# Token shift by ScalarE into PSUM, squares of the input norms in PSUM, the projection's low parts read back from DRAM, and a new order

## The chip, the cores and the metric

The kernel runs on one core of a Trainium2 chip. Five engines run their own instruction streams: TensorE (PE, with PEld for its weight loads), VectorE (DVE), ScalarE (ACT), GpSimd (POOL) and SyncE (SP), which issues the transfers of this kernel; sixteen DMA engines carry them out. The metric is the device time of one launch in microseconds (us). Three runs of the kernel before gave 2299.95, 2302.5 and 2308.67 us; their median is 2302.5 us.

## The reference

One layer of a hybrid decoder, for 1024 prompt tokens and 8 decode tokens that share the weights. D_MODEL is 1024, D_FF 2816, all in fp32. Cut to the parts in question:

```python
h = x + 0.5 * rmsnorm(swiglu(rmsnorm(x, n_ffn1_pre), ffn1_gate, ffn1_up, ffn1_down), n_ffn1_post)
u = rmsnorm(h, n_mix_pre)
proj = u @ w_in                       # 26 column tiles of 128
...                                   # group A: differential attention
shifted = concatenate([prev, pb[:, :-1]])
xs = pb + (shifted - pb) * mu_shift   # token shift of group B
...                                   # group B: RWKV-7 delta rule, 8 heads of 64
h = h + rmsnorm(concatenate([ya, yb]) @ w_out, n_mix_post)
h = h + 0.5 * rmsnorm(swiglu(rmsnorm(h, n_ffn2_pre), ffn2_gate, ffn2_up, ffn2_down), n_ffn2_post)
```

## The kernel before, in words

Activations stand transposed, features on partitions and tokens on the free axis. The tokens are worked in two halves of about 512. There are four FFN phases, called trunk0 to trunk3: trunk0 and trunk1 are the first FFN of halves 0 and 1, trunk2 and trunk3 the second FFN of halves 0 and 1. Between them lie, for each half, the input projection `proj` (w_in, 26 column tiles), the mixing work (`job`, `lora`, `attn`, `prep`, `fin`), the output projection (`out` for half 0, `outb` for half 1), and norms: a phase's `tail` is the norm and residual after it, `outn` the one after the output projection, `stats` and `pre` the one ahead of an FFN. `dec` and `decb` are the decode tokens' attention and state update; `decb` reads its state and operands as 64x512 pieces from DRAM (`decb_dreg<-Dd`).

Each fp32 product is three matmuls (`mm3`, L675): high weight by high input, high weight by low input, low weight by high input. `split` (L599) makes the two parts of a weight tile: ACT casts the high part, and DVE or POOL subtracts it from the raw tile for the low part. With `kept` the low part is written to DRAM in half 0 and read from there in half 1, in place of the subtraction (`aside`, L615). Before, this is done for parts of the FFN weights and for w_out (`Lo`), named in `LOWS` (L99). The projection's tiles use buffers w0 and w1 in half 0, and w2 and w3, taken in turn, in half 1; a tile's buffer is given to the tile after the next when its last matmul is done. In half 1 a tile is 24 matmuls of 512 columns; of each three, the third needs the low part.

`stats` (L794) sums the squares of eight feature tiles: ACT squares into a buffer `sqs` (one buffer), DVE or POOL adds it to an accumulator, a matmul with ones sums over the partitions, ACT takes the root and DVE the reciprocal (`rstd`). The token shift (in `s_mix`'s streams) is a POOL subtraction of a 128x512 tile and a DVE multiply-add.

The order is not the program's. Generators ("streams") put instructions; `Kern.run` (L475) lists them for each engine by earliest start, ties by a late time, and every engine then runs its list in that order. The late times come from dry passes (`latest`, L564): each pass runs the list, works back from its end, and gives the next pass its late times; `PASSES` is how many. `BIAS` moves the late times of a stream by a number of microseconds. Since all engine work is issued through one helper, every row of the profile has its line, L317 (L320 after); streams are told apart by the tiles' names. PSUM banks: trunk uses m0 and m1, projections m2 and m3, norms a small bank "dec" or "aux".

## Time and profile before

The profiled execution took 2294.3 us, its span 2292.3; that is 8.2 us (0.36%) under the median of the three runs.

| engine | busy, us | share of the span |
|---|---|---|
| PE | 2228.0 | 97% |
| PEld | 1985.3 | 87% |
| DVE | 1556.5 | 68% |
| ACT | 1078.0 | 47% |
| POOL | 1021.6 | 45% |

The rows of the trace give an engine's instructions in order of time with, in brackets, the idle time ahead of one and what ended it. PEclk is the granted TensorE clock as a share of the full one. The DMA share is the mean busy share of the sixteen DMA engines. Idle time of an engine other than PE costs nothing by itself.

### The profile page before, as it was taken

What the parts mean: (1) busy time and instruction counts of PE and PEld (TensorE: products, weight loads), DVE (VectorE), ACT (ScalarE), POOL (GpSimd) and SP (SyncE); (2) the same over time, 40 slices, a digit from 0 to 9 for tenths busy, and PEclk for the clock granted to TensorE, in tenths of its full rate; (3) what the DMA queues carried; (4) which work ended last, traced back from release to release, by engine and by line L of the source; (5) the groups of instructions that cost most, each with busy time, mean ns of one, the idle gap of its engine ahead of it and who ended that gap; (6) DMA issues with size and microseconds to landing.
All of it is one profiled execution on the core that took longest, in us unless ns stands there. A gap on an engine that the chain in (4) does not pass through costs nothing. (4 is left out here: it accounts for less than half of the span.)

```text
span 2292.3 us, 42829 instructions
## 1 busy us (share of the span) xinstructions
PE 2228.0 (97%) x15857; PEld 1985.3 (87%) x15857; DVE 1556.5 (68%) x3545; ACT 1078.0 (47%) x2231; POOL 1021.6 (45%) x846
## 2 busy tenths in 40 slices
PE   8999999999999999999899999999999999999998
PEld 7999999799887778988787867777788888999998
DVE  5477988756766687477866367665667356777776
ACT  5433443634354365434552145443665556544444
POOL 3344565534343566356543124333443254544443
PEclk9999999999999999999899999999999999999999
DMA  6423334344334576655679643324745847544543
GB/s 205 132 86 100 102 93 130 104 146 140 109 113 108 170 228 204 218 151 151 194 200 225 169 138 114 111 75 121 205 122 168 273 145 249 148 114 130 148 138 111
DMA packets 476295, 343.15 MB, mean 150 GB/s; under 512 B 82457, under 2 KB 424061, under 8 KB 476088
## 3 DMA queue, kind: packets, MB, share of 16 engines
q1 hardware_dynamic: 475480, 338.82, 50.8%
q8 instruction: 125, 2.05, 0.4%
q0 software_dynamic: 320, 1.08, 0.1%
q14 instruction: 82, 0.67, 0.1%
q10 hardware_dynamic: 288, 0.52, 0.1%
HBM read 278.98 MB, written 61.38 MB: 148 GB/s over the span
## 5 line engine op out<-in xcount | busy, mean ns | idle before, releaser
L317 PE MATMUL trunk_m<-trunk_xl,wts_w 128*128 128x256 f32 (+2 forms) x2700 | 459.4, 321 | 6.9 <-DVE trunk_xl L317 6.2
L317 POOL TENSOR_TENSOR wts_w<-wts_raw,wts_w 128x1024 fp32r<-128x1024 f32 (+2 forms) x162 | 314.4, 1948 | 318.1 <-ACT wts_w L317 279.4
L317 PE MATMUL trunk_m<-pre_X,wts_w 128*128 128x512 f32 (+3 forms) x2400 | 439.9, 335 | 5.7 <-POOL wts_w L317 2.8
L317 PEld LDWEIGHTS trunk_m<-trunk_xl,wts_w 128*128 128x128 f32 x2700 | 382.3, 189 | 42.3 <-DVE trunk_xl L317 7.9
L317 PEld LDWEIGHTS trunk_m<-pre_X,wts_w 128*128 128x128 f32 x2400 | 352.6, 190 | 48.2 <-issue 6.8
L317 PE MATMUL trunk_m<-pre_T,wts_w 128*128 128x512 f32 (+3 forms) x1848 | 362.8, 347 | 5.2 <-DVE trunk_xl L317 2.4
L317 ACT CAST wts_w<-wts_raw 128x1024 fp32r<-128x1024 f32 (+2 forms) x293 | 244.2, 848 | 237.9 <-PE trunk_m L317 162.1
L317 PEld LDWEIGHTS trunk_m<-pre_T,wts_w 128*128 128x128 f32 x1848 | 286.9, 190 | 43.7 <-issue 3.8
L317 DVE TENSOR_TENSOR trunk_xl<-trunk_xl,trunk_m 128x256 f32<-128x256 f32 (+2 forms) x351 | 165.8, 489 | 77.3 <-PE trunk_m L317 76.1
L317 PE MATMUL proj_m<-tail_xl,lin_w 128*128 128x256 f32 (+1 forms) x1248 | 168.5, 290 | 2.3 <-POOL lin_w L317 1.9
L317 PEld LDWEIGHTS proj_m<-tail_xl,lin_w 128*128 128x128 f32 x1248 | 155.6, 190 | 11.3 <-issue 7.0
L317 POOL TENSOR_TENSOR trunk_xl<-trunk_t,trunk_xl 128x512 fp32r<-128x512 f32 (+3 forms) x86 | 94.5, 1100 | 149.9 <-ACT trunk_xl L317 149.7
L317 PE MATMUL proj_m<-tail_T,lin_w 128*128 128x512 f32 (+1 forms) x672 | 153.1, 386 | 4.9 <-ACT tail_T L317 3.8
L317 PEld LDWEIGHTS proj_m<-tail_T,lin_w 128*128 128x128 f32 x672 | 122.6, 192 | 33.2 <-ACT tail_T L317 4.2
L317 DVE TENSOR_TENSOR wts_w<-wts_raw,wts_w 128x1024 fp32r<-128x1024 f32 (+2 forms) x101 | 108.1, 1071 | 35.1 <-ACT wts_w L317 34.4
L317 POOL TENSOR_TENSOR wts_w<-wts_lraw,wts_w 128x512 fp32r<-128x512 f32 x44 | 66.4, 1512 | 53.5 <-ACT wts_w L317 46.9
L317 ACT CAST wts_w<-wts_lraw 128x512 fp32r<-128x512 f32 x94 | 55.9, 617 | 64.7 <-DMA wts_lraw<-in_ffn_down_dram 33.4
L317 POOL TENSOR_TENSOR lin_w<-lin_raw,lin_w 128x1024 fp32r<-128x1024 f32 x19 | 45.9, 2417 | 79.4 <-ACT lin_w L317 69.7
L317 DVE TENSOR_TENSOR trunk_t<-trunk_g,trunk_m 128x512 f32<-128x512 f32 (+2 forms) x75 | 42.1, 562 | 53.4 <-PE trunk_m L317 50.7
L317 POOL TENSOR_TENSOR mix_T<-mix_T 128x512 f32<-128x512 f32 x32 | 38.6, 1207 | 79.2 <-DMA mix_T<-PT 54.6
L317 PE MATMUL trunk_aux<-trunk_xl,wts_w 128*128 128x256 f32 (+1 forms) x516 | 71.5, 283 | 0.0
L317 PE MATMUL trunk_m<-comb_T,wts_w 128*128 128x260 f32 x540 | 69.8, 283 | 0.0
(645 smaller groups left out, 4273.9 us busy)
## 6 DMA issues: line engine op xcount, KB each, us to landing
wts_raw<-in_ffn_gate_dram SPq DMA_DIRECT2D x88, 512.0 KB
wts_raw<-in_ffn_up_dram SPq DMA_DIRECT2D x58, 512.0 KB
wts_raw<-in_ffn_down_dram SPq DMA_DIRECT2D x56, 384.0 KB
wts_raw<-in_ffn_down_dram SPq DMA_DIRECT2D x29, 512.0 KB
lin_raw<-in_w_in_dram SPq DMA_DIRECT2D x26, 512.0 KB
wts_w<-Ld SPq DMA_DIRECT2D x22, 512.0 KB
mix_T<-PT SPq DMA_DIRECT2D x37, 256.0 KB
Ld<-wts_w SPq DMA_DIRECT2D x24, 384.0 KB
```

Of the source, the lines that this page charges most:

```text
L317: o = Op(eng, lambda: fn(*a, **k), st)
```

## The change

Six things change. (1) `PASSES` goes from 2 to 4, and the `BIAS` table loses ten entries and gets two; so every engine's order may change. (2) `MIX`: the token shift's first half is an ACT instruction that writes (1 - mu) times the tile into PSUM, and DVE adds mu times the shifted tile to it; POOL's subtraction is gone. A small tile `rest_mu` is computed once. (3) `SQP`: `stats` writes its squares into a PSUM tile and adds all of them on DVE. (4) `LOWS` has "in": the projection's 26 low parts (512 KB each) are written to DRAM in half 0 (`Li<-lin_w`) and read in half 1 (`lin_w<-Li`), in place of 26 subtractions. (5) The stream `lora` is given the PSUM bank "dec". (6) `SWAP` is 0, so its branches do nothing.

```diff
-PASSES = 2
-BIAS = {"trunk2": 310, "outn3": -60, "outb0": 30, "pre2": -3, "outn0": -30, "rows0": -30, "job00": -10, "job03": 10, "stats0": 10, "dec0": 10, "wts3": 3, "pre3": -30, "mix1": -60, "lora1": 3, "attn11": 3, "tail2": 3}
+PASSES = 4
+BIAS = {"trunk2": 300, "outn3": -60, "outb0": 30, "pre2": -3, "pre1": -60, "rope0": 10}
 SHIFT = {}
+SWAP = 0
+MIX = 1
+SQP = 1
...
-LOWS = (1, "out")
+LOWS = (1, "in", "out")
...
+        self.rest_mu = self.T(self.const, [P, NB], "rmu")
+        nc.vector.tensor_scalar(self.rest_mu, self.vecs("mu_shift"), -1.0, 1.0, ALU.mult, ALU.add)
...
         for k in range(KT):
-            self.square_sum(rb, src[k], k, self.tmp(*tmp, rb.shape[-1]), **kw)
+            if SQP:
+                self.square_sum(rb, src[k], k, self.ps2()[:, :rb.shape[-1]], engines=("vector",))
+            else:
+                self.square_sum(rb, src[k], k, self.tmp(*tmp, rb.shape[-1]), **kw)
         self.rstd(rb)
...
-        self.spawn(self.s_lora(pool, half), "lora", 0)
+        self.spawn(self.s_lora(pool, half), "lora", 0, "dec")
...
+        if MIX:
+            part = self.ps2()
+            nc.scalar.activation(part, E[:, 1:], AF.Copy, scale=self.rest_mu[:, m:m + 1])
+            nc.vector.scalar_tensor_tensor(out, E[:, 0:HS], self.vec("mu_shift", m), part, ALU.mult, ALU.add)
+            return
         nc.gpsimd.tensor_tensor(out, E[:, 0:HS], E[:, 1:], ALU.subtract)
         nc.vector.scalar_tensor_tensor(out, out, self.vec("mu_shift", m), E[:, 1:], ALU.mult, ALU.add)
```

Counted over the whole program, PE has the same 14542 matmuls of the same shapes, in another order. DVE goes from 3537 to 3560 instructions, ACT from 2097 to 2108, POOL from 851 to 790, and SP issues 1323 transfers where it issued 1271: 26 writes and 26 reads more.

Where the order moves, three places matter below.

**From trunk1 to the projection of half 1.** TensorE before: the last matmuls of trunk1's down product (into trunk_m), the tail's sum over partitions (tail_aux), the first matmul of the projection (proj_m), the decode matmuls (decb_dec).

```order
L317 MATMUL trunk_m0_1501_12945<-trunk_xl1_955_8277,wts_w1_1467_12797 128x256 x5
L317 MATMUL tail_aux0_1477_12868<-trunk_acc_1445_12646,init_onesD_3_76 128x256
L317 MATMUL trunk_m0_1501_12945<-trunk_xl1_955_8277,wts_w1_1467_12797 128x256 x4
L317 MATMUL proj_m3_1524_12976<-tail_T0_1482_12873,lin_w2_1520_12972 128x256
L317 MATMUL decb_dec_1455_12712<-decb_dreg_1454_12711,bset_wa_56_159 128x8
L317 MATMUL decb_dec_1455_12712<-decb_dreg_1454_12711,bset_g2_57_160 128x8
```

TensorE now, at the same place, in two pieces: the end of trunk1, and the first matmul of the projection. Between the first and the last row of the two stand 48 matmuls of trunk2 (from pre_X) and the second tail's sum (tail_aux1).

```order
L320 MATMUL trunk_m0_1516_13007<-trunk_xl1_969_8303,wts_w1_1482_12863 128x256 x9
L320 MATMUL decb_dec_1457_12629<-decb_dreg_1455_12627,bset_wa_57_160 128x8 x2
L320 MATMUL tail_aux0_1492_12928<-trunk_acc_1464_12724,init_onesD_3_76 128x256
L320 MATMUL trunk_m1_1545_13053<-pre_X0_1372_11671,wts_w0_1512_12976 128x256
L320 MATMUL trunk_m1_1545_13053<-pre_X1_1373_11672,wts_w0_1512_12976 128x256
```

```order
L320 MATMUL trunk_m0_1548_13085<-pre_X0_1372_11671,wts_w1_1518_13018 128x256 x2
L320 MATMUL tail_aux1_1520_13020<-trunk_acc_1465_12725,init_onesD_3_76 128x256
L320 MATMUL trunk_m0_1548_13085<-pre_X1_1373_11672,wts_w1_1518_13018 128x256
L320 MATMUL trunk_m0_1548_13085<-pre_X0_1372_11671,wts_w1_1518_13018 128x256 x2
L320 MATMUL trunk_m0_1548_13085<-pre_X1_1373_11672,wts_w1_1518_13018 128x256
L320 MATMUL trunk_m0_1548_13085<-pre_X0_1372_11671,wts_w1_1518_13018 128x256
L320 MATMUL proj_m3_1539_13040<-tail_T0_1497_12933,lin_w2_1535_13036 128x256
```

Four trunk matmuls stood between the tail's sum and the projection's first; now 48 do. Another 48 of 256 columns and 11 of 512 columns stand between that first matmul and the projection's second, and the decode matmuls have moved ahead of the tail's sum.

**The projection of half 1.** SP's queue before, in the middle of it: loads of raw tiles (lin_lraw, lin_LT), of the decode update's pieces (decb_dreg), stores of results (PT).

```order
L317 DMA decb_dreg_12711<-in_state_wkv_dram 64x8x64 x2
L317 DMA decb_dreg_12711<-Dd 64x8x64 x5
L317 DMA PT<-init_E_115 128x512
L317 DMA decb_dreg_12711<-Dd 64x8x64
L317 DMA lin_lraw_13820<-in_w_in_dram 128x8x128
L317 DMA PT<-init_rb_114 128x512
L317 DMA lin_LT_13879<-in_w_in_dram 128x8x128
L317 DMA decb_dreg_12711<-Dd 64x8x64 x4
```

The same queue now, at the like place:

```order
L320 DMA lin_w_1634_13903<-Li 128x1024
L320 DMA decb_dreg_12627<-Dd 64x8x64
L320 DMA PT<-init_rb_114 128x512
L320 DMA decb_dreg_12627<-Dd 64x8x64 x3
L320 DMA lin_LT_13936<-in_w_in_dram 128x8x128
L320 DMA decb_dreg_12627<-Dd 64x8x64
L320 DMA lin_w_1637_13935<-Li 128x1024
```

Every tile has a read of its low part more, issued among the decode update's reads and waiting for its buffer.

**From the output projection of half 1 to trunk3.** TensorE before: behind the last matmul of outb come trunk2's last down products of 512 columns and then whole gate products of trunk2 (from pre_X) around outn's sum (outn_aux).

```order
L317 MATMUL outb_m2_2304_19724<-outb_T0_2194_18739,lin_w3_2301_19649 128x256
L317 MATMUL trunk_m1_2259_19330<-trunk_xl1_955_8277,wts_w1_2241_19161 128x512 x4
L317 MATMUL trunk_m0_2261_19346<-trunk_xl1_955_8277,wts_w1_2241_19161 128x512 x9
L317 MATMUL trunk_m1_2284_19440<-pre_X0_1352_11509,wts_w0_2252_19260 128x512
L317 MATMUL trunk_m1_2284_19440<-pre_X1_1353_11510,wts_w0_2252_19260 128x512
```

TensorE now, from outn's sum on: trunk2's last down products, the transposes of results (rows_cb), and the sum of pre3's norm (stats_dec).

```order
L320 MATMUL outn_aux1_2361_20021<-bset_sg_65_168,init_onesD_3_76 128x256
L320 MATMUL trunk_m1_2352_19868<-trunk_xl1_969_8303,wts_w1_2334_19692 128x256 x3
L320 MATMUL trunk_m0_2355_19911<-trunk_xl1_969_8303,wts_w1_2334_19692 128x256 x9
L320 MATMUL trunk_m1_2359_19987<-trunk_xl1_969_8303,wts_w0_2305_19569 128x256 x9
L320 MATMUL trunk_m0_2400_20108<-trunk_xl1_969_8303,wts_w0_2305_19569 128x256 x9
L320 MATMUL rows_cb_2375_20035<-init_ident_1_69,outb_T2_2257_19018 128x128 x4
L320 MATMUL trunk_m1_2404_20127<-trunk_xl1_969_8303,wts_w1_2334_19692 128x256 x6
L320 MATMUL rows_cb_2376_20036<-init_ident_1_69,outb_T3_2258_19019 128x128 x2
L320 MATMUL trunk_m1_2404_20127<-trunk_xl1_969_8303,wts_w1_2334_19692 128x256 x3
```

outb now ends later against trunk2: 19 matmuls of 256 columns stand between its last and outn_aux1 (20 of 512 columns before), and behind this piece come trunk_m0_2406 (9), stats_dec, 16 transposes, and trunk_m1_2410.

DVE before, at the end of pre3's norm, between pre3's multiplies (into pre_T) and the evacuations of trunk2's down products (trunk_xl0 from trunk_m):

```order
L317 SCALAR_TENSOR_TENSOR pre_T1_2322_19785<-pre_sq_2334_19797,setup_cols_49_152,pre_T0_2321_19784 128x256
L317 SCALAR_TENSOR_TENSOR pre_T1_2322_19785<-pre_sq_2335_19798,setup_cols_49_152,pre_T0_2321_19784 128x256
L317 TENSOR_TENSOR trunk_xl0_1588_13641<-trunk_xl0_1588_13641,trunk_m1_2366_20121 128x256
L317 SCALAR_TENSOR_TENSOR pre_T1_2322_19785<-pre_sq_2336_19799,setup_cols_49_152,pre_T0_2321_19784 128x256
L317 COPY rows_X0_2347_20053<-rows_cb_2353_20059 128x512
L317 TENSOR_TENSOR trunk_xl0_1588_13641<-trunk_xl0_1588_13641,trunk_m0_2368_20137 128x256
```

DVE now:

```order
L320 SCALAR_TENSOR_TENSOR pre_T1_2383_20058<-pre_sq_2396_20071,setup_cols_49_152,pre_T0_2382_20057 128x256
L320 SCALAR_TENSOR_TENSOR pre_T1_2383_20058<-pre_sq_2397_20072,setup_cols_49_152,pre_T0_2382_20057 128x256
L320 TENSOR_TENSOR pre_sq_2398_20073<-outb_T3_2258_19019,bset_bv1_71_174 128x256
L320 SCALAR_TENSOR_TENSOR pre_T1_2383_20058<-pre_sq_2398_20073,setup_cols_49_152,pre_T0_2382_20057 128x256
L320 SCALAR_TENSOR_TENSOR pre_T1_2383_20058<-pre_sq_2399_20074,setup_cols_49_152,pre_T0_2382_20057 128x256
L320 TENSOR_TENSOR trunk_acc_2337_19709<-trunk_acc_2337_19709,trunk_sq_2401_20117 128x256
L320 TENSOR_TENSOR trunk_xl0_1589_13543<-trunk_xl0_1589_13543,trunk_m1_2404_20127 128x256
```

Before, the evacuations stood among pre3's multiplies; now that of trunk_m1_2404, which frees the bank for trunk_m1_2410, stands behind all of them.

More of the change, by code (lines that the diff above doesn't have):

```diff
@@ L1941, in s_decode_a @@
         yield ("wait", "lead")
+        if SWAP:
+            yield ("wait", "decb")
         yield from self.a_decode()
-        self.spawn(self.s_decode_b(), "decb", 1, "dec", ahead=8)
+        if SWAP:
+            self.signal("dec_b")
+        else:
+            self.spawn(self.s_decode_b(), "decb", 1, "dec", ahead=8)
     def s_decode_b(self):
         yield ("wait", "proj0")
+        if SWAP:
+            yield ("wait", "setup")
+            yield ("wait", "lead")
         take = self.arena(self.T(self.pool, [P, W_DEC], "dreg"))
         yield from self.b_decode(take, take, take(TD, C))
-        self.signal("dec_b")
+        self.signal("decb" if SWAP else "dec_b")
     def s_states(self, pool):
@@ L2581, in hymba_kernel @@
     K.spawn(K.s_decode_a(), "dec", 1, "cb", ahead=24)
+    if SWAP:
+        K.spawn(K.s_decode_b(), "decb", 1, "dec", ahead=8)
     K.run()
```

## Prediction

> **What bounds the kernel.** I read the page's first part, then TensorE's waits, then the stretches of 100 us in which TensorE is not full, then TensorE's rows there.
>
> ```profile
> PE 2228.0 (97%) x15857; PEld 1985.3 (87%) x15857; DVE 1556.5 (68%) x3545; ACT 1078.0 (47%) x2231; POOL 1021.6 (45%) x846
> ```
>
> TensorE is busy for 2228.0 of 2292.3 us. Its matmuls do not change, so only its 64 us without work, and the time at a lower clock, can.
>
> ```profile
> 0.00:100.00 100.00, 89.31 (x688) 86.62 (x689) 49.96 (x132) 54.59 (x110) 36.91 (x39) 0.97 0.56 178
> 300.00:400.00 100.00, 96.00 (x773) 94.54 (x773) 83.36 (x170) 41.68 (x87) 54.85 (x45) 0.98 0.42 122
> 400.00:500.00 100.00, 94.33 (x619) 85.61 (x619) 70.92 (x111) 49.06 (x79) 47.53 (x49) 0.98 0.42 126
> 1100.00:1200.00 100.00, 91.25 (x588) 82.62 (x587) 72.28 (x146) 53.49 (x101) 53.87 (x53) 0.93 0.67 190
> 1800.00:1900.00 100.00, 93.13 (x605) 84.54 (x604) 47.63 (x77) 52.01 (x93) 44.44 (x53) 0.97 0.68 206
> 1900.00:2000.00 100.00, 96.59 (x788) 95.58 (x787) 66.91 (x130) 57.28 (x116) 49.10 (x55) 0.98 0.62 188
> ```
>
> Columns: stretch, length, busy time of PE, PEld, DVE, ACT, POOL, then the granted clock, DMA share, GB/s. The first stretch is the start, whose order begins alike. That leaves three seams: trunk0 to the first projection (300 to 500 us, 9.7 us without work), trunk1 to the second (1100 to 1200, 8.75 us), and outb to trunk3 (1800 to 2000, 10.3 us).
>
> **1. Trunk1 to the second projection.** TensorE's rows, with idle time in brackets, and the granted clock there:
>
> ```profile
> 1128.90 0.59 PE L317 MATMUL tail_aux<-trunk_acc,init_onesD 128*128 128x256 f32 x2
> 1129.14 0.82 PE L317 MATMUL trunk_m<-trunk_xl,wts_w 128*128 128x256 f32 x4
> 1133.71 0.58 PE L317 MATMUL proj_m<-tail_T,lin_w 128*128 128x256 f32 x1 [3.76 <-ACT tail_T L317]
> 1137.28 0.59 PE L317 MATMUL decb_dec<-decb_dreg,bset_wa 64*128 64x8 f32 x2 [2.99 <-ACT decb_dreg L317]
> 1141.14 5.08 PE L317 MATMUL proj_m<-tail_T,lin_w 128*128 128x256 f32 x21 [1.17 <-DVE tail_T L317]
> ```
>
> ```profile
> 1133.20:1146.80 13.60, 8.93 (x36) 8.27 (x36) 9.24 (x19) 7.75 (x18) 7.61 (x11) 0.50 0.82 268
> ```
>
> Behind the tail's sum the chain is root, reciprocal, multiply, add, high part: 4.8 us from 1128.90 to 1133.71, with 0.82 us of matmuls beside it. The three gaps are 7.92 us, and 8.93 us of matmuls ran at half clock, which cost half of that, 4.5 us: 12.4 together. Now 48 trunk matmuls lie in the chain's shadow. They take .130 us each (the row at 1909.06 below: 4.55 us for 35), 6.2 us, more than 4.8; the decode matmuls that waited for ACT stand earlier, and 48 of 256 and 11 of 512 columns (.236 each, below) follow the first projection matmul, 8.8 us in which the other seven tiles of the tail come. What may remain: waits for the low part of trunk2's first weights and for bank evacuations. For those I take 3 us: the trunk waits of before were 2.53 and 1.52 us (below). The step gains 9.4 us; at best 12.4, at worst 5 (two such waits and a half-clock window).
>
> The Trainium skill ("TensorE: Matmul & The Clock Gate", Part 1) says that after a window of about 3.4 us without enough work the clock is halved, whatever the single waits are. The trace agrees: 13.6 us, four such windows, at 0.50 here. By it the 4.5 us go whole if no gap here passes some 3 us; the sum has it so anyway.
>
> **2. outb to trunk3.** TensorE's gaps and the rows that price the chain:
>
> ```profile
> 1841.88 4.47 PE L317 MATMUL outb_m<-outb_T,lin_w 128*128 128x256 f32 x24 [2.10 <-DMA lin_w<-Lo]
> ...
> 1858.99 3.17 PE L317 MATMUL trunk_m<-trunk_xl,wts_w 128*128 128x512 f32 x13
> ...
> 1863.62 0.59 PE L317 MATMUL outn_aux<-bset_sg,init_onesD 128*128 128x256 f32 x2
> ...
> 1875.84 0.60 PE L317 MATMUL rows_cb<-init_ident,outb_T 128*128 128x128 f32 x4
> 1876.19 1.07 PE L317 MATMUL trunk_m<-pre_X,wts_w 128*128 128x256 f32 x7
> 1879.79 5.81 PE L317 MATMUL trunk_m<-pre_X,wts_w 128*128 128x256 f32 x34 [2.53 <-POOL wts_w L317]
> 1885.50 0.70 PE L317 MATMUL stats_dec<-bset_bv,init_onesD 128*128 128x256 f32 x2
> ...
> 1891.10 0.66 PE L317 MATMUL rows_cb<-init_ident,outb_T 128*128 128x128 f32 x4 [0.68 <-ACT rows_X L317]
> ...
> 1895.60 0.66 PE L317 MATMUL rows_cb<-init_ident,outb_T 128*128 128x128 f32 x4 [0.83 <-ACT rows_X L317]
> ...
> 1909.06 4.55 PE L317 MATMUL trunk_m<-trunk_xl,wts_w 128*128 128x256 f32 x35 [1.52 <-DVE trunk_xl L317]
> ...
> 1918.20 7.01 PE L317 MATMUL trunk_m<-pre_T,wts_w 128*128 128x264 f32 x43 [1.89 <-ACT trunk_sq L317]
> ```
>
> ```profile
> 1867.36 3.21 DVE L317 SCALAR_TENSOR_TENSOR outb_T<-outb_T,setup_cols,outn_aux 128x256 f32<-128x256 f32 x8
> ...
> 1882.84 0.42 DVE L317 TENSOR_TENSOR bset_bv<-bset_bv,stats_sqs 128x256 f32<-128x256 f32 x1 [0.30 <-ACT stats_sqs L317]
> ...
> 1886.88 1.75 DVE L317 RECIPROCAL bset_bv<-bset_bv 128x256 f32<-128x256 f32 x1 [1.15 <-ACT bset_bv L317]
> 1888.55 0.92 DVE L317 TENSOR_TENSOR wts_w<-wts_raw,wts_w 128x768 fp32r<-128x768 f32 x1
> ...
> 1892.69 0.48 DVE L317 SCALAR_TENSOR_TENSOR pre_T<-pre_sq,setup_cols,pre_T 128x256 fp32r<-128x256 f32 x1
> ```
>
> ```profile
> 1881.62 0.74 POOL L317 TENSOR_TENSOR bset_bv<-bset_bv,stats_sqs 128x256 f32<-128x256 f32 x1
> ```
>
> Before, outn's sum (1863.62) had 22 us of trunk2 matmuls behind it until pre3's sum (1885.50), and pre3's chain another 33 us until trunk3 (1918.20). In the new order the whole chain must pass before trunk2's last six products, since DVE evacuates trunk_m1_2404 behind the last multiply of pre3. DVE's work from outn_aux1 to pre3's last add: reciprocal 1.75, eight multiplies 3.2, seven adds of squares 2.9, five pre_T multiplies 2.4, five trunk instructions 2.1, one add .4, one weight subtraction .9: 13.7 us. Then the sum .7, root .5, reciprocal 1.75, twelve more instructions at .48 (5.7), and the evacuation .8: 23.2 us. Beside it TensorE has 48 matmuls (6.2 us) and six groups of transposes at .35 (1876.19 less 1875.84; 2.1), with the sums 8.9 us. 14.3 us are left uncovered. Ahead of it outn's sum came 4.6 us after outb's last matmul (1863.62 less 1858.99, where the trunk matmuls behind it start); 19 trunk matmuls now cover 2.5 of that, leaving 2.1. Trunk3's start costs the 1.52 and 1.89 again. Together 19.8 us, against 7.45 before without the 2.10 for the low part of w_out (2.53 + .68 + .83 + 1.52 + 1.89): +12.4. Against that, DVE's instructions in this list may partly run while outb still does, and SQP takes adds from POOL (.74 us in the last row, where DVE takes .42). I take +10, plus 1 for another half-clock window, +11; ends 0 (all of the chain runs ahead of the seam) and +18 (every handoff costs .3 us more over some twenty).
>
> **3. The projection of half 1.** What a tile takes, the price of a read, and the DMA load:
>
> ```profile
> L317 PE MATMUL proj_m<-tail_T,lin_w 128*128 128x512 f32 x576 | 135.7, 396 | 0.0
> ```
>
> ```profile
> 1834.32 0.44 SPq L317 DMA_DIRECT2D lin_w<-Lo  x1
> ...
> 1841.87 4.17 PEld L317 LDWEIGHTS outb_m<-outb_T,lin_w 128*128 128x128 f32 x24 [2.53 <-DMA lin_w<-Lo]
> ```
>
> ```profile
> 1240.07 0.66 SPq L317 DMA_DIRECT2D lin_lraw<-in_w_in_dram  x1
> ...
> 1246.72 1.05 ACT L317 CAST lin_w<-lin_lraw 128x1024 fp32r<-128x1024 f32 x1 [6.37 <-DMA lin_lraw<-in_w_in_dram]
> ```
>
> ```profile
> 1175.00:1280.00 105.00, 102.77 (x454) 81.59 (x453) 70.64 (x102) 31.86 (x42) 37.35 (x23) 1.00 0.97 242
> 1280.00:1310.00 30.00, 30.00 (x131) 24.26 (x130) 8.44 (x10) 5.69 (x6) 4.05 (x2) 1.00 0.43 140
> ```
>
> A matmul is 135.7/576 = .236 us, a tile of 24 is 5.65. TensorE never waited here (0.0), though each tile's low part cost DVE or POOL a subtraction; those were off the path, so dropping them gains nothing. New is that a tile's low part can be read only when the tile two before is done. It must land within one tile and two matmuls, 5.65 + .47 = 6.1 us; later by d costs d once in two tiles. A read of 512 KB took 7.55 us from issue (1834.32) to the weight load that waited for it (1841.87), and 6.65 (1240.07 to 1246.72) in this stage. The loss per tile is then .27 to .72 us. Some 16 of the 24 tiles lie in the stretch where the DMA engines are 0.97 busy with the decode update's reads: 4 to 12 us. Outside it, at 0.43, I count none. The order puts 51 trunk matmuls (12 us) in small groups behind the second matmul of these tiles, in the place of the wait; I take 5. Ends: 0, and the case below.
>
> By the Trainium skill ("DMA: Bandwidth & Descriptors", Anatomy of one DMA) a transfer costs about 2.0 us and its bytes at 436 GB/s; that estimate is 3.2 us here, and the sum would lack these 5 us. The two rows contradict it under load.
>
> **4. The rest.** The first seam (300 to 500 us): the first tail's sum stands one product earlier, POOL's subtraction of the projection's low parts stays: -1, from -4 to +3, since the 9.7 us are many waits, the longest of them this:
>
> ```profile
> 406.76 5.83 PE L317 MATMUL trunk_m<-pre_T,wts_w 128*128 128x256 f32 x47 [2.43 <-DVE trunk_xl L317]
> ```
>
> The 26 writes of half 0: the price of 512 KB is .43 x 30 us / 4.2 MB (140 GB/s x 30 us) = 3.07 us of all engines per MB, 1.6 each, 42 us over half 0's projection, beside a share of 0.42: hidden; at most .15 x 26 = 4 us where a buffer waits for its write. MIX: POOL's 28 subtractions become 28 ACT instructions, and DVE reads PSUM; the jobs that use the tiles are a step shorter or as long: 0, -2 to +2, the cover being projection and trunk matmuls.
>
> ```profile
> L317 POOL TENSOR_TENSOR mix_T<-mix_T 128x512 f32<-128x512 f32 x32 | 38.6, 1207 | 79.2 <-DMA mix_T<-PT 54.6
> L317 ACT ACTIVATE mix_T<-mix_T 128x512 f32<-128x512 f32 x36 | 22.7, 631 | 31.2 <-DVE mix_T L317 30.3
> ```
>
> SQP elsewhere: 0, since no wait of TensorE above is for the sums of `stats`.
>
> **Sum.** -9.4 + 11 + 5 - 1 = +5.6 us. The profiled execution, 2294.3 us, becomes 2299.9; the median of the three runs, 8.2 us higher, 2302.5 to 2308. What a measurement here can tell from no change is 0.5%, 11.5 us: 2291 to 2314.
>
> **Rivals.** (a) The second projection is bound by the DMA engines. Sixteen reads at 1.6 us are 26 us of all engines in a stretch with 3 us free; 23 us are left, 11 if the 12 us of trunk matmuls there lengthen it. For it: 0.97. Against it: outb's reads lived beside 206 GB/s and more with 2.10 us lost at most. At 17 instead of 5: 2320, slower; it decides once the reads take over 7.5 us on average. (b) The third seam is covered: if outn's and pre3's work runs ahead, step 2 is 0 and the rest stands: 2297; with no loss in step 3 as well 2292, and with step 1 at its best 2289, faster. For it: DVE was busy for 47.63 of 100 us there. Against: each link waits for the one before. (c) The reads land as fast as without load, by the skill's rule too: 2303. (d) The third seam is as bad as its end, with half clock through it: +18 to +25, 2316 to 2322.
>
> **Chances.** The forecast .45, (a) .22, (b) .15, (c) .10, (d) .08. Slower: most of (a) and (d) and .04 of the forecast, .33. Faster: less than half of (b) and the best ends of the others, .12. Same: .55. The range leaves out the best ends of (b) and the worst of (a): 2293 to 2324; the forecast alone 2299 to 2316.
>
> **What would show it.** Step 1: gaps ahead of the first proj_m after trunk1 under 3 us and no run of half clock. Step 2: a wait of TensorE for trunk_xl of some 7 us, near the transposes before trunk3. Step 3: waits of proj_m for the low part's read, some .3 us each on every second tile while the decode update reads. Wrong it would be if the reads' waits pass 15 us, or if outn's sum comes far ahead of trunk2's last products in time.

## The result, and the profile after

Over eleven runs each on the same chip the changed kernel has a median of 2302.03 us (2298.62 to 2310.42) and the kernel before one of 2301.42 us (2294.27 to 2308.67): a ratio of 1.0008, with a 95% interval of 0.9993 to 1.0023. That is no change that can be told. The profiled execution of the changed kernel took 2298.98 us, its span 2297.2, against 2294.3 and 2292.3 before. The profiled execution of before lay 7.1 us under its median of eleven and that of after 3.0 under its own, so 4.1 of the 4.9 us between the two spans are scatter between executions. Differences of under some 3 us in one stretch are therefore not read below. Two executions far out, one of the kernel before (3549 us) and one of the parts with the old settings (12271 us, below), are left out of the medians and ratios.

The page's first part, after:

```profile
PE 2229.2 (97%) x15857; PEld 1983.2 (86%) x15857; DVE 1515.4 (66%) x3568; ACT 1090.1 (47%) x2242; POOL 955.0 (42%) x785
```

The sums hide that TensorE's idle time has moved. Stretches of the kernel before, then the same stretches after (columns as in the prediction: stretch, length, busy PE, PEld, DVE, ACT, POOL, granted clock, DMA share, GB/s):

```profile
300.00:500.00 200.00, 190.33 (x1390) 180.15 (x1390) 154.28 (x280) 90.74 (x166) 102.38 (x94) 0.98 0.42 124
1110.00:1160.00 50.00, 41.58 (x290) 39.35 (x290) 36.79 (x78) 30.48 (x61) 28.20 (x32) 0.86 0.62 178
1160.00:1330.00 170.00, 167.44 (x769) 134.93 (x767) 92.36 (x141) 47.54 (x65) 53.78 (x36) 1.00 0.75 197
1860.00:1945.00 85.00, 77.50 (x554) 72.90 (x553) 54.01 (x100) 51.22 (x91) 41.49 (x50) 0.96 0.58 180
```

```profile
300.00:500.00 200.00, 194.46 (x1448) 184.05 (x1447) 144.26 (x288) 92.64 (x169) 100.46 (x86) 1.00 0.48 149
1110.00:1160.00 50.00, 47.76 (x340) 44.37 (x341) 39.36 (x74) 30.31 (x56) 32.01 (x29) 1.00 0.76 240
1160.00:1330.00 170.00, 166.84 (x757) 133.96 (x756) 66.21 (x123) 55.37 (x76) 23.92 (x19) 1.00 0.96 264
1860.00:1945.00 85.00, 65.62 (x463) 60.17 (x463) 45.43 (x89) 47.62 (x88) 36.16 (x45) 0.86 0.54 168
```

Length less PE's busy time is the time without work. With it I count what half clock costs, half of the matmul time inside the windows at clock 0.5, and call the two the lost time:

| stretch, us | before | after |
|---|---|---|
| 300 to 500 (first seam) | 13.1 | 5.5 |
| 500 to 1110 | 5.5 | 11.4 |
| 1110 to 1160 (second seam) | 12.9 | 2.2 |
| 1160 to 1330 (second projection) | 2.6 | 3.2 |
| 1330 to 1780 | 9.2 | 9.0 |
| 1780 to 1945 (third seam) | 15.4 | 27.7 |

What the first two seams gain, 18.3 us, the third and the stretch from 500 to 1110 give back: 12.3 and 5.9. The rows sum to 0.3 us more than before. Over the whole span the time without work grew by 3.7 us (64.3 to 68.0) and the cost of half clock fell by 5.6 (16.0 to 10.4). What made the span 4.9 us longer is TensorE's busy time apart from half clock, 2212.1 us before and 2218.8 after, for the same matmuls; no run here shows why, or whether that is scatter.

The second seam after, TensorE's rows:

```profile
1130.87 0.70 PE L320 MATMUL tail_aux<-trunk_acc,init_onesD 128*128 128x256 f32 x2
1131.22 0.59 PE L320 MATMUL trunk_m<-pre_X,wts_w 128*128 128x256 f32 x2
1133.07 5.13 PE L320 MATMUL trunk_m<-pre_X,wts_w 128*128 128x256 f32 x41 [1.26 <-POOL wts_w L320]
...
1139.05 0.34 PE L320 MATMUL proj_m<-tail_T,lin_w 128*128 128x256 f32 x1
1139.91 5.95 PE L320 MATMUL trunk_m<-pre_X,wts_w 128*128 128x256 f32 x48 [0.52 <-DVE trunk_g L320]
```

No wait for tail_T is left, the longest gap is 1.26 us, and the granted clock is 1.00. The third seam after, TensorE's rows and then two of VectorE's:

```profile
1873.97 2.40 PE L320 MATMUL trunk_m<-trunk_xl,wts_w 128*128 128x256 f32 x19
1876.21 0.59 PE L320 MATMUL outn_aux<-bset_sg,init_onesD 128*128 128x256 f32 x2
...
1883.97 0.33 PE L320 MATMUL rows_cb<-init_ident,outb_T 128*128 128x128 f32 x1 [1.07 <-POOL outb_T L320]
...
1899.41 1.02 PE L320 MATMUL rows_cb<-init_ident,outb_T 128*8 128x128 f32 x4 [0.67 <-ACT rows_X L320]
1908.10 8.76 PE L320 MATMUL trunk_m<-trunk_xl,wts_w 128*128 128x256 f32 x51 [7.67 <-DVE trunk_xl L320]
...
1921.00 3.64 PE L320 MATMUL trunk_m<-pre_T,wts_w 128*128 128x264 f32 x26 [1.19 <-ACT wts_w L320]
```

```profile
1906.30 1.07 DVE L320 SCALAR_TENSOR_TENSOR pre_T<-pre_sq,setup_cols,pre_T 128x256 fp32r<-128x256 f32 x2 [0.58 <-ACT pre_T L320]
...
1907.63 0.42 DVE L320 TENSOR_TENSOR trunk_xl<-trunk_xl,trunk_m 128x256 f32<-128x256 f32 x1
```

The 7.67 us are the bank that VectorE evacuates only behind pre3's last multiplies, as the prediction read it from the order.

The second projection after: SyncE's issues of two reads, then TensorE's rows that wait for them.

```profile
1242.02 0.77 SPq L320 DMA_DIRECT2D lin_w<-Li  x1
...
1270.83 1.00 SPq L320 DMA_DIRECT2D lin_w<-Li  x1
```

```profile
1248.62 5.83 PE L320 MATMUL proj_m<-tail_T,lin_w 128*128 128x512 f32 x24 [0.83 <-DMA lin_w<-Li]
...
1276.72 16.95 PE L320 MATMUL proj_m<-tail_T,lin_w 128*128 128x512 f32 x72 [0.95 <-DMA lin_w<-Li]
```

From issue to the matmul that waited it is 6.60 and 5.89 us, in a stretch whose DMA share is 0.96. In the whole kernel these waits are five (total, times, longest, in us):

```profile
PE proj_m L320 <- DMA lin_w<-Li: 3.0, 5, 1.0
```

The Trainium skill ("DMA: Bandwidth & Descriptors", Anatomy of one DMA) gives 2.0 us and the bytes at 436 GB/s as a fit for transfers that GpSimd issues; the prediction took it for these reads, which SyncE issues, an estimate of 3.2 us. The two rows have about twice that.

### The profile page after: what moved, and what is told of

It is laid out like the page before. It is cut to its first block, busy times and chain, and to the rows that moved or that the text cites. A ratio compares the mean times of both kernels' runs of the same rounds, so it can differ in the third digit from the quotient of the medians.

```text
span 2297.2 us, 42866 instructions
## 1 busy us (share of the span) xinstructions
PE 2229.2 (97%) x15857; PEld 1983.2 (86%) x15857; DVE 1515.4 (66%) x3568; ACT 1090.1 (47%) x2242; POOL 955.0 (42%) x785
## 4 chain that ended last, share of the span: by engine, by line
PE 55%; DMA 7%; DVE 5%; ACT 3%; issue 2%; SPq 2%; POOL 1%; DVEq 0%; ACTq 0%; POOLq 0%
PE trunk_m L320 32%; PE proj_m L320 5%; PE trunk_aux L320 5%; PE job_aux L320 5%; PE out_m L320 2%; PE attn_m L320 2%; SPq L320 2%; PE outb_m L320 2%; PE attn_aux L320 2%; DMA decb_dreg<-Dd 1%; DMA lin_w<-Lo 1%; DMA out_dram<-decb_dreg 1%; DVE trunk_xl L320 1%; ACT wts_w L320 1%; ACT mix_T L320 1%
## 5 line engine op out<-in xcount | busy, mean ns | idle before, releaser
L320 POOL TENSOR_TENSOR wts_w<-wts_raw,wts_w 128x1024 fp32r<-128x1024 f32 (+2 forms) x169 | 330.8, 1965 | 421.0 <-ACT wts_w L320 339.3
L320 PE MATMUL trunk_m<-trunk_xl,wts_w 128*128 128x256 f32 (+2 forms) x2700 | 464.5, 323 | 15.6 <-DVE trunk_xl L320 11.8
L320 PEld LDWEIGHTS trunk_m<-trunk_xl,wts_w 128*128 128x128 f32 x2700 | 384.3, 191 | 52.9 <-DVE trunk_xl L320 15.4
L320 DVE TENSOR_TENSOR wts_w<-wts_raw,wts_w 128x1024 fp32r<-128x1024 f32 (+2 forms) x94 | 97.8, 1041 | 32.6 <-ACT wts_w L320 31.0
L320 POOL TENSOR_TENSOR lin_w<-lin_raw,lin_w 128x1024 fp32r<-128x1024 f32 x23 | 56.4, 2454 | 113.8 <-ACT lin_w L320 95.6
L320 POOL TENSOR_TENSOR wts_w<-wts_lraw,wts_w 128x512 fp32r<-128x512 f32 x43 | 59.9, 1396 | 44.8 <-ACT wts_w L320 41.4
L320 ACT CAST trunk_xl<-trunk_t 128x512 fp32r<-128x512 f32 (+2 forms) x101 | 48.9, 484 | 41.9 <-DVE trunk_t L320 41.3
L320 DVE SCALAR_TENSOR_TENSOR trunk_g<-trunk_t,trunk_m 128x512 f32<-128x512 f32 (+2 forms) x52 | 32.4, 624 | 53.0 <-ACT trunk_t L320 52.7
```

The lines of the kernel that those rows point to most:

```text
L320: o = Op(eng, lambda: fn(*a, **k), st)
```

## The experiments

All ratios are to the kernel before, run on the same chip; the changed kernel stands at 1.0008. "Held" means that the changed kernel's own order is written down in its last dry pass, as a list of instructions with the engine each was given, and listed again word for word while a part is taken out; "planned anew" means that the dry passes ran with the edit. Lost times are from one trace of each kernel, ratios from all its runs.

### The shared buffer ahead of trunk3

The products of pre3 (`pre_sq`) use the buffer `sq`, two deep, which trunk2's own activations use as well. Here they get one of their own, one deep:

```diff
-                    t = self.tmp("sq", 2, n) if ph == 3 else src[k]
+                    t = self.tmp("sqs", 1, n) if ph == 3 else src[k]
```

> Only pre3's scaled tiles get a buffer of their own, in place of the two that trunk2's squares use too. Theory A (the 7.67 us wait ahead of trunk3 comes from trunk2's evacuations queueing behind pre3's multiplies on DVE, through these two buffers): the wait falls under 2 us, trunk3 starts 6 to 8 us sooner after outn's sum, the time is 6 to 10 us below the changed kernel's (about 2293). Rival B (trunk2 has too few matmuls left by then, and trunk3 waits for the end of pre3 whatever the buffers are): the wait moves to trunk3's first matmul, the time stays within 2 us of the changed kernel's.

Measured: 2293.47 us (12 runs), before 2299.42; 0.9985 [0.9970, 1.0000]. TensorE around the wait:

```profile
1895.61 5.51 PE L320 MATMUL trunk_m<-trunk_xl,wts_w 128*128 128x256 f32 x43
1900.95 0.59 PE L320 MATMUL last_aux<-trunk_acc,init_onesD 128*128 128x256 f32 x2
1901.19 1.88 PE L320 MATMUL trunk_m<-trunk_xl,wts_w 128*128 128x256 f32 x13
1909.80 4.09 PE L320 MATMUL trunk_m<-pre_T,wts_w 128*128 128x264 f32 x20 [6.73 <-DVE trunk_xl L320]
```

The evacuations now stand among pre3's multiplies and trunk2's last products run ahead of the wait. The wait does not go: 6.73 us of it stand ahead of trunk3's first matmul, as rival B had it. But trunk3 starts at 1909.8 instead of 1921.0, with outn's sum where it was (1876.3 and 1876.2). The stretch from 1860 to 1945 loses 19.0 us instead of 26.5, and the time is some 5 us under the changed kernel's, short of theory A's 6 to 10 and past rival B's 2. TensorE's order is the changed kernel's, row for row, up to 1849 us, so the gain belongs to this seam. What is left of the wait ends with an evacuation that VectorE reaches 6 us after trunk2's products in front of it are done (1903.1), with no idle time between:

```profile
1902.38 1.75 DVE L320 RECIPROCAL last_aux<-trunk_acc 128x256 f32<-128x256 f32 x1
...
1904.37 2.42 DVE L320 SCALAR_TENSOR_TENSOR trunk_xl<-trunk_xl,setup_cols,last_aux 128x256 f32<-128x256 f32 x6
...
1909.25 0.41 DVE L320 TENSOR_TENSOR trunk_xl<-trunk_xl,trunk_m 128x256 f32<-128x256 f32 x1
```

So some 7 us of the seam came from the order that the shared buffer forced. The rest stands behind VectorE's own list (trunk2's last norm, pre3's last multiplies and two sums for trunk3); no run changes that list alone.

The same with one more pass of the planner:

```diff
-PASSES = 4
+PASSES = 5
```

> The same buffer and one more planning pass (5 in place of 4); the order moves from half 1's work on. Theory A: the wait ahead of trunk3 is gone as with 4 passes, and more of trunk2's matmuls are left behind outb; 8 to 15 us below the kernel before (about 2288). Rival B: as the changed kernel, 2300 to 2304.

Measured: 2293.6 us (10 runs); 0.9976 [0.9964, 0.9988]. The seam loses 19.6 us. The fifth pass made no difference that can be told from the fourth, and the 5.5 us under the kernel before are short of theory A's 8.

### The reads, out of a held order

Half 1's low parts are subtracted again behind each cast, by VectorE or GpSimd; the writes of half 0 stay.

```diff
-                               [(self.Li[m], half == 0) for m in ms] if "in" in LOWS else None)
+                               [(self.Li[m], half == 0) for m in ms] if "in" in LOWS and (READ or not half) else None)
...
+    Kern.tape = ...      # the order held, a subtraction behind each cast, no reads
+    globals().update(dict(READ=0))
```

> The changed kernel's own order, held fixed, but in half 1 the projection's low parts are subtracted by DVE or POOL again, not read from DRAM (the writes of half 0 stay). Theory (the reads cost little: TensorE's waits for them are 3.0 us in all): 0 to 5 us below the changed kernel, about 2299, with the waits for Li gone and the first job matmul of half 1 (1233) starting a few us sooner. Rival (the DMA engines bind that stage, and the reads delay half 1's whole chain): 10 us or more below, with the decode update's end (1393) and the jobs' start back near those before (1332 and 1209).

Measured: 2308.43 us (6 runs), before 2299.42; 1.0043 [1.0027, 1.0060]: some 8 us slower than with the reads, which neither the theory nor the rival had. TensorE's order is the same row for row; from 1000 to 1330 us it loses 18.0 us instead of 8.1. TensorE's waits from 1110 to 1330:

```profile
PE trunk_m L322 <- POOL wts_w L322: 3.1, 2, 2.8
PE tail_aux L322 <- DVE init_rb L322: 3.1, 1, 3.1
PE trunk_m L322 <- DVE trunk_g L322: 1.2, 1, 1.2
PE proj_m L322 <- DVE tail_T L322: 0.9, 1, 0.9
```

The waits for the reads are gone, and waits for VectorE and GpSimd have come: the weights' low parts, the tail and the bank evacuations stand behind the subtractions. In this order the subtractions were not free. The reads had not delayed what follows either: without them the jobs of half 1 start later, at 1246.9 instead of 1233.3 us.

### The order alone, the parts alone

First the new `PASSES` and `BIAS` without MIX, SQP and the projection's low parts (the bank of `lora` stays "dec"), planned anew:

```diff
-MIX = 1
-SQP = 1
+MIX = 0
+SQP = 0
...
-LOWS = (1, "in", "out")
+LOWS = (1, "out")
```

> The new planning (4 passes, the new table) without the three new mechanisms: the token shift on POOL, squares in SBUF, projection's low parts subtracted. Theory (the seams move with the order, the mechanisms as such cost and give next to nothing): 2295 to 2310, with the first seam (300 to 500 us) as short of idle time as in the changed kernel (some 5 us), whichever of the later seams gets it back. Rival (the mechanisms make the gain at the first seam): there 12 us or more are lost, as before.

Measured: 2309.94 us (10 runs), before 2299.42; 1.0036 [1.0018, 1.0054]. (The table loses twelve entries, not ten, gets two, and `trunk2` goes from 310 to 300.) The first seam loses 7.4 us where the kernel before lost 13.1 and the changed one 5.5: most of that gain comes with the order. The second seam loses 7.1, the third 12.9 (1860 to 1945), and the long stretches between them more than before (8.0 from 1160 to 1330, 7.1 from 1500 to 1780, against 2.6 and 1.6).

Then all parts with the old planner settings:

```diff
-PASSES = 4
-BIAS = {"trunk2": 300, "outn3": -60, "outb0": 30, "pre2": -3, "pre1": -60, "rope0": 10}
+PASSES = 2
+BIAS = {"trunk2": 310, ...}      # the table of before
```

> The three mechanisms with the old planning (2 passes, the old table). In its order only 60 matmuls of trunk2 stand between outb's last and trunk3's first, where the changed kernel has 139 and the kernel before 302. Theory (the third seam is paid by what of trunk2 is left): about 79 matmuls of .13 us less cover than in the changed kernel, 10 us more lost between 1860 and 1945 us, 2305 to 2320. Rival (the mechanisms as such make the kernel faster, the planning costs): 2297 or less.

Measured: 2323.19 us (5 runs), before 2301.11; 1.0093 [1.0066, 1.0121], above the theory's 2320 at its end. Only 60 matmuls of trunk2 are left when outb ends, and TensorE waits:

```profile
1908.30 1.33 PE L320 MATMUL trunk_m<-trunk_xl,wts_w 128*128 128x256 f32 x9 [1.74 <-DVE trunk_xl L320]
1921.20 1.09 PE L320 MATMUL last_aux<-init_ident,trunk_xl 128*128 128x128 f32 x4 [11.56 <-DVE trunk_xl L320]
```

Last the changed kernel without the projection's low parts, planned anew:

```diff
-LOWS = (1, "in", "out")
+LOWS = (1, "out")
```

> The changed kernel with LOWS without 'in', planned anew: the projection's low parts are subtracted in half 1, and the planner may place them. In its order 265 matmuls of trunk2 are left behind outb. Theory from the last runs (reading spares DVE and POOL work at the seam from trunk1 to the projection, worth 5 to 9 us there): the second seam loses 5 us or more again, the third is short (under 16 us lost), 2298 to 2306. Rival (the read is worth nothing once the order is free): the second seam stays under 4 us, and the time is 2293 or less.

Measured: 2295.99 us (12 runs), before 2301.11; 0.9979 [0.9962, 0.9995], between the theory's range and the rival's. The second seam loses 6.2 us instead of 2.2, as the theory had it, the third (1860 to 1945) 18.9 instead of 26.5, the projection (1160 to 1330) 2.6 instead of 3.2, and the stretch from 500 to 1110 20.5 instead of 11.4. These do not add up to a gain: the two profiled executions are 1 us apart (2297.95 and 2298.98), and the 7 us stand between the medians alone, so no stretch can be named for them.

These make a chain, each kernel planned for itself: the order (with the bank of `lora`) 1.0036 (+8 us), MIX and SQP added 0.9979 (13 us less), the low parts added 1.0008 (7 us more). Along this path the change is a loss, a gain and a loss that cancel. Each step also plans the order anew (TensorE's order differs from the changed kernel's from 442 us on with the order alone, from 478 us on without the low parts), so its number is that of a part with the order it gets. Along the other path the signs turn: all parts with the old settings are 21 us slower than the kernel before, and the new settings then gain 20. What the runs show is that parts and order cannot be priced apart.

### MIX and SQP out of the held order

```diff
+    Kern.tape = Kern.taped[0]      # the order held
+    globals().update(dict(MIX=0))
```

> The changed kernel's own order, held fixed, with the token shift as before: POOL subtracts, DVE multiplies and adds, all in SBUF. Theory (hidden): within 2 us of the changed kernel's 2302. Rival (the tiles stand at the head of half 1's chain of jobs, and POOL's 1.2 us for ACT's 0.6 delays it): the first job matmul of half 1 comes 1 us or more later and the time is 3 us or more above.

Measured: 2315.79 us (6 runs), before 2301.11; 1.0067 [1.0043, 1.0091], 14 us over the changed kernel. TensorE's waits from 440 to 600 us, in half 0's jobs:

```profile
PE job_dec L321 <- DVE mix_T L321: 5.6, 2, 3.8
```

In the changed kernel the same waits are 0.7 us. TensorE's order is the same row for row, and from 300 to 1000 us it loses 26.7 us instead of 14.2, most of the 14. The token shift does stand on a path, but not first where the rival had it: GpSimd's subtraction ahead of VectorE's multiply-add delays the tile that the first jobs of half 0 wait for. Half 1's first job matmul then comes 12 us later too (1245.2 instead of 1233.3).

```diff
+    Kern.tape = Kern.taped[0]
+    globals().update(dict(SQP=0))
```

> The changed kernel's order, held fixed, with the squares of the input norms in SBUF again (one buffer), the adds left on DVE. Theory (hidden, and one PSUM tile or one SBUF buffer gives the same chain): within 2 us of the changed kernel's 2302, the wait ahead of trunk3 still 7 to 8 us. Rival (PSUM shortens the chain of squares and adds ahead of pre3): that chain is longer by 1 us or more per norm, the time 3 us or more above.

Measured: 2329.4 us (6 runs), before 2301.11; 1.0115 [1.0087, 1.0143]. The order could not be held at the second seam (TensorE's rows differ from 1138 to 1162 us), since the tail's squares take the shared buffer `sq` again:

```profile
1153.46 0.28 PE L321 MATMUL proj_m<-tail_T,lin_w 128*128 128x256 f32 x1
1161.97 7.84 PE L321 MATMUL proj_m<-tail_T,lin_w 128*128 128x256 f32 x47 [8.23 <-DVE tail_T L321]
1172.15 0.70 PE L321 MATMUL tail_aux<-trunk_acc,init_onesD 128*128 128x256 f32 x2 [2.34 <-POOL trunk_acc L321]
```

So it prices a buffer that stops the tail as much as the squares. The next run therefore leaves the tail's squares in PSUM and takes only those ahead of the second FFN back, and there TensorE's order held to the last row:

```diff
-            if SQP:
+            if SQP or tmp[0] == "sq":
...
+    globals().update(dict(SQP=0))
```

> The changed kernel's order, held fixed on every engine, with the squares in SBUF only for the norms ahead of the second FFN; the tails' squares stay in PSUM. Theory (what cost 27 us in the run without SQP was that the tail's squares went back into the two buffers that trunk2 uses, at the second seam): within 3 us of the changed kernel's 2302. Rival (the chain of squares ahead of pre3 is what PSUM makes short): 2310 or more, the loss between 1860 and 1945 us larger by 5 or more.

Measured: 2309.24 us (7 runs), before 2296.77; 1.0054 [1.0034, 1.0074], 11 us over the changed kernel. The stretch from 1860 to 1945 loses 29.4 us instead of 26.5, less than the rival's 5 us more, and from 1000 to 1110, where half 0's squares are summed, 10.3 instead of 2.7. Both are places where these instructions stand, and ScalarE's squares wait 15.5 us in all for VectorE's adds, where they waited 9.4 in PSUM. But no wait of TensorE from 1000 to 1110 names the squares, and 4.7 of the 10.3 us there are half clock; so that the 11 us come by this chain is argued from the places. The first 100 us, where the two orders are alike, differ by 5 us, which is scatter.

### Two orders that could not be held

MIX alone in the order of the kernel before, with the bank "dec" for `lora`:

```diff
-MIX = 0
+MIX = 1
...
-        self.spawn(self.s_lora(pool, half), "lora", 0)
+        self.spawn(self.s_lora(pool, half), "lora", 0, "dec")
```

> The kernel before in its own order, but with the token shift by ACT into PSUM (and the lora stream in the bank that this needs, which moves some of the jobs' small matmuls). Theory (an order is fitted to the lengths it was planned with: taking MIX out of the new order cost 14 us, putting it into the old one gives nearly nothing): within 4 us of the kernel before. Rival (MIX is worth its 14 us anywhere): 10 us or more below the kernel before.

Measured: 2345.57 us (4 runs), before 2296.77; 1.0205 [1.0181, 1.0229]. Nothing expected this. One wait in the second projection is most of it; TensorE's row, then VectorE's groups from 1264 to 1299 us:

```profile
1297.70 1.19 PE L321 MATMUL proj_m<-tail_T,lin_w 128*128 128x512 f32 x2 [29.19 <-DVE init_E L321]
```

```profile
L321 DVE TENSOR_TENSOR decb_dreg<-decb_dreg 128x512 f32<-128x512 f32 x14 | 9.8, 700 | 25.9 <-DMA decb_dreg<-Dd 25.6
```

With MIX the token shift of `lora` takes a PSUM tile, here of the bank that the decode update uses, and the decode update's next matmuls moved back (from 1154.7 and 1177.8 us before, to 1226.9 and 1257.1 here). Its reads from DRAM were issued late and in bunches, and VectorE, whose list was held, waited 25.6 us for them in several waits with the evacuation of the projection's bank behind. That the shared bank moved those matmuls is read from the rows; it was not tried by itself. The first seam loses 14.7 us here and 13.1 before: MIX without the new order gains nothing there. Another 15 us are lost from 500 to 1110 us (20.8 instead of 5.5), where rows of half 0's jobs moved too, from 475 us on; no run takes that apart. So the run prices an order that was broken in several places, the delay of the decode most of all, and not the token shift.

To test whether trunk2's matmuls are one store of filler, they were held back by hand in the changed kernel's order:

```diff
+    gone = set(i for i in spots if base[i][1] < HOLD + 52)      # trunk2's places from 1162 us on
+    more = [first + (j + 0.5) * (last - first) / 52 for j in range(52)]      # from outn's sum to pre3's end
+    places = sorted([i for i in spots if i not in gone] + more)
```

> The order of the changed kernel is held, but from a point in the second projection on (1162 us) every instruction of trunk2's stream stands 52 of that stream later, 48 of them matmuls; the last 52 are spread over the stretch from outn's sum to the last multiply of pre3. Theory: the trunk2 matmuls are one store of filler, and what the second seam used is lacking at the third. Then the 11 us of matmuls taken out of the projection bring half 1's jobs forward by some 10 us (first job 1222 where it was 1233), and the third seam (1780 to 1945 before, now some 10 us sooner) loses 14 to 20 us where it lost 27.6: 0.996 to 0.999 of the kernel before, 4 to 10 us under the changed kernel. Rival: the matmuls covered something where they stood; new waits of 5 us or more come up between 1160 and 1250, and the time is that of the changed kernel, 1.000 to 1.003. Second rival: a held order whose parts are moved by hand costs more than the parts, as the held orders before this one did: over 1.004.

Measured: 2468.42 us (6 runs), before 2298.62; 1.0744 [1.0715, 1.0772]. The second projection and half 1's jobs in this kernel, then in the changed one:

```profile
1160.00:1345.00 185.00, 172.36 (x760) 136.73 (x760) 69.75 (x130) 49.88 (x68) 20.70 (x17) 0.98 0.93 245
1345.00:1725.00 380.00, 316.72 (x2019) 237.18 (x2018) 192.75 (x583) 141.41 (x286) 100.98 (x67) 0.91 0.32 89
```

```profile
1160.00:1345.00 185.00, 181.84 (x821) 146.06 (x820) 72.40 (x133) 58.29 (x81) 26.60 (x22) 1.00 0.93 257
1345.00:1630.00 285.00, 280.76 (x2015) 217.12 (x2014) 185.19 (x584) 139.71 (x282) 100.29 (x66) 1.00 0.42 118
```

The second rival came, at 1.0744. The 48 matmuls had covered something where they stood: the projection does not end sooner, and TensorE idles 12.6 us there instead of 3.2. Then the jobs take 380 us instead of 285 for the same matmuls, in many waits of up to 5 us, since every trunk product in between now stands at another place than the jobs' waits. The test says nothing on the store; it says what a shift of one stream by 52 instructions costs.

### Both repairs together

```diff
-PASSES = 4
+PASSES = 5
...
-LOWS = (1, "in", "out")
+LOWS = (1, "out")
...
-                    t = self.tmp("sq", 2, n) if ph == 3 else src[k]
+                    t = self.tmp("sqs", 1, n) if ph == 3 else src[k]
```

> All three findings together: pre3's own buffer, no reads of the projection's low parts, one planning pass more (5). Theory (the second seam's filling and the third seam's wait are separate, and both can be short): under 4 us lost between 1110 and 1160 us and under 20 between 1860 and 1945, half 1's chain early, 2283 to 2291, under the kernel before by 10 us or more. Rival (what is saved at one seam is paid at the other): 2293 to 2297, as the runs with one finding each.

Measured: 2292.11 us (12 runs), before 2296.77; 0.9976 [0.9959, 0.9993]. With the own buffer and five passes alone it was the same 0.9976. Both lie some 5 us under the kernel before and 7 under the changed one; the two repairs do not add. The two stretches are as short as the theory had them, 0.4 and 11.5 us, but 5 us came instead of 10 or more; from 500 to 1110 the kernel loses 19.0 us, where the changed one loses 11.4.

### What the runs have in common at the third seam

Planned orders only; lost time from 1860 to 1945 us, and the matmuls of trunk2 that come behind outb's last and ahead of trunk3's first, counted in the traces:

| kernel | ratio | left | lost, us |
|---|---|---|---|
| before | 1 | 301 | 10.9 |
| the order alone | 1.0036 | 302 | 12.9 |
| own buffer, no low parts, five passes | 0.9976 | 265 | 11.5 |
| no low parts | 0.9979 | 265 | 18.9 |
| own buffer, five passes | 0.9976 | 160 | 19.6 |
| changed | 1.0008 | 139 | 26.5 |
| own buffer | 0.9985 | 130 | 19.0 |
| the parts with the old settings | 1.0093 | 60 | 38.1 (to 1954) |

The more of trunk2 was spent earlier, the more is lost here. The own buffer takes about 7 us off at either number of matmuls. That is a relation over eight orders; no run moved the filler and nothing else, and the ratios do not follow it: the order alone loses little here and is slower.

## Why the prediction was right, and where it was not

The forecast was 2308 us in a range of 2293 to 2324, with most of the chance on no change; 2302.0 came out, and a ratio of 1.0008. By steps:

**Step 1, the second seam: right.** Forecast 9.4 us gained, measured 10.7 (12.9 less 2.2). The 48 matmuls stand beside the chain, one wait for the low part of trunk2's first weights is left (1.26 us), and half clock is gone.

**Step 2, the third seam: right in place and in its total, with a chain that was too short.** Forecast 11 us lost, measured 12.3 from 1780 to 1945. The wait for trunk_xl of some 7 us near the transposes is there with 7.67, and the granted clock of 0.86 over those 85 us (24 us at half clock) is more than the one window counted. That rules out rival (b). But from outn's sum to the release of the bank (1876.21 to 1908.05) it took 31.8 us where the sum of VectorE's instructions gave 23.2: VectorE was busy for 23.1 of them, so its work was counted nearly right, and the waits in between were left out. TensorE's work beside it was 15.7 us, not 8.9: there was more of it, and over half of it ran at half clock. So 16.2 us were left uncovered where 14.3 were forecast. The two errors nearly cancel, which is luck. What the step also lacked is a second cause: it took the list of VectorE as given, while 7 us of the loss hang on one shared buffer.

**Step 3, the projection of half 1: mis-sized at its place, and with a false premise.** Forecast 5 us of waits for the reads, .3 us each on every second tile; they are 3.0 in all, five waits of 0.2 to 1.0, and the stretch loses only 0.6 us more than before. Rival (a), the DMA bound, fell with it: at a DMA share of 0.96 and above the reads came at most 1 us late. The premise that dropping the subtractions gains nothing, since TensorE never waited for them, is wrong in the new order, where putting them back cost 8 us. And when the low parts are left out and the kernel is planned anew, 7 us are gained, but with waits for the reads of only 3.0 to save, and at no stretch that the traces can name. So the 5 us of step 3 are near what the part costs by luck, and its reason was not right. Rival (c), 2303, is the nearest of all to the measured time, and again not by its reason: the two reads shown took 6.60 and 5.89 us, so they were not fast; they had time.

**Step 4, the rest: wrong in two terms.** The first seam was to gain 1 us, from -4 to +3; it gained 7.6, mostly by the order (5.7 with the order alone). MIX and SQP were put at 0. They are worth 13 us together in kernels planned for them, and in the held order 14 us for MIX and 11 for SQP ahead of the second FFN. The step failed where it took "no wait of TensorE is for this" as "nothing stands behind this": in the new order GpSimd's subtraction stands ahead of 5.6 us of TensorE's waits. For ScalarE's squares into one buffer the like is argued, not shown. And no term at all was for the stretch from 500 to 1110 us, which loses 5.9 us more; its cause stays open.

**The sum.** +5.6 us forecast, about +2 measured (0.08% of 2301). By parts the forecast for the order (steps 1, 2 and the first seam) was +0.6, and the order alone is +8; for MIX and SQP 0, and it is -13; for the low parts +5, and it is +7 (by the path above; by the other one the parts are a loss). That the result lies within 6 us of the forecast is in good part luck, since these cancel, and the two seams that the prediction priced were right only for the order that all parts together make. The premise that only TensorE's 64 us without work and its half clock can change did not hold either: these two fell by 1.9 us together, while the profiled span grew by 4.9.

## What to carry to other kernels

Where TensorE's gaps are filled from one supply of spare matmuls, a filled gap is not yet a gain: count what is left of the supply at the last place that needs it, and read that place first (here a relation over eight orders, not shown by itself). A list order fits the lengths and buffers it was planned with, so a part taken out of it, or a stream moved in it, can cost far more than the part (8 to 47 us here, 169 at worst); compare kernels that are each planned anew, change one thing from one to the next, and try a second path before adding the parts up. Look for scratch buffers and PSUM banks that two independent chains share, since the order can be bound there without any wait naming it.

## What was not expected of the hardware

A DMA share of 0.96 over 170 us made the reads at most 1 us late: the two shown took 6.60 and 5.89 us from issue to use, where 6.65 and 7.55 had been seen before. And in the kernel before with MIX, VectorE's waits for bunches of small reads, 25.6 us in all, became one wait of 29.2 us of TensorE, since the evacuation stood behind them in VectorE's list; the clock was at half for 30.7 us from 1272 on.
